# The norm of x in a fused block: its squares behind the casts of V's weights, its additions on Pool

## The chip, the core and the metric

The kernel runs on one core of a Trainium2 chip. The time is the device time of one execution in microseconds. The kernel before took 879.01 us (median of three runs, 878.78 to 880.6). A core has five engines that run side by side, each through its own queue in order: TensorE (matrix products; PE in the profile, with its weight loads as PEld), VectorE (DVE), ScalarE (ACT), GpSimd (Pool, POOL) and SyncE (SP), which here only issues loads. Semaphores make an engine wait for another.

## The reference, cut to what matters

The reference is one layer of a streaming encoder on 512 frames of width 1024, in float32. Two mixers (RWKV-7 and a gated linear recurrence) read one input projection of the normalised x; a cross-attention into a fixed memory of 256 rows and a gated convolutional feed-forward layer follow. What the change touches is at the very front:

```python
def rms_norm(x, g):
    xf = x.astype(jnp.float32)
    y = xf * lax.rsqrt(jnp.mean(xf * xf, axis=-1, keepdims=True) + NORM_EPS)
    return (y * g.astype(jnp.float32)).astype(x.dtype)
...
h = rms_norm(x, norm_mix_g[l])
proj = h @ w_in[l] + b_in[l]
...
kv = m @ w_kv          # m = rms_norm(mem, norm_mem_g[l])
```

The input projection has 38 column blocks of 128 (`w_in`). K and V of the cross-attention depend only on the memory, so the kernel computes them first, while x and its norm are made ready. The low-rank matrices `w_lora_up` and `a_lora_up` are read by the RWKV branch.

## The kernel before, in words

All activations lie transposed: 128 channels on the partitions, frames along the free axis. x is `xraw`, 8 blocks of 128 x 512. Products keep float32 accuracy with three passes of a faster type: every operand is split into a high part (a cast on ScalarE, names ending in `_h` or index 0) and a low part (what the cast left over, a subtraction on VectorE, `_l` or index 1), and `mm3` (L232) multiplies high by high, high by low and low by high into one accumulator.

Weights come in tiles of 128 x 1024 (512 KB). `stream` (L160) issues a load on SyncE's queue, casts the tile on ScalarE (L176) and subtracts on VectorE (L177). There are four buffers for raw tiles and three each for high and low parts, so a load waits for a raw buffer, and everything behind it in SyncE's queue waits too.

The front of the program runs so:

1. The memory `mraw` is loaded, scaled and split into `m2`. K's eight blocks (`k_ps0` to `k_ps7`, 24 products of 256 columns each) are multiplied with eight tiles of `wk`. Two blocks share one accumulator bank, and `k_out` (L415) reads a block from it, scales it by the norm of the memory and hands it to Pool for a store to `dK`. So the last block waits until the block before it has been read.
2. x is loaded in four pieces of two blocks (L428), the pieces standing between weight loads in SyncE's queue. When the norm of the memory is due (after K's block 5), `m_norm` computes it with a refinement step on VectorE (`newton`, L328).
3. The squares of x: ScalarE squares each block (L441, L444), VectorE adds it to `xss` (L445). Two buffers hold squares.
4. V: two halves of 512 columns, each with four tiles of `wv` and 48 products of 512 columns (L465). Between the halves, in program order, stands `x_norm` (L446): `rstd_bc` splits `xss` into two parts (`rx_h`, `rx_l`, by `sum_exact`, L223), sums both over the partitions with a product by ones (`rs_ps`), and ScalarE takes logarithm and exponential to get `rx`, the reciprocal root. Then every block becomes a row of the projection's operand: VectorE multiplies x, its gain and `rx` (L451, `hf32`), ScalarE casts (L452, `h2` high) and VectorE subtracts (L453, `h2` low; `hT` in the profile).
5. The input projection starts with blocks 12 and 13 (L659, L668), whose products run as rows of `h2` come. Between them are the casts and subtractions of two low-rank matrices (L666, L667), which the first low-rank products need much later. A chain of small operations on 128 x 4 tiles (`dp`, L478 to L521) runs on VectorE in the same stretch.

What sets the order: a planner orders each engine's queue before the program runs. It goes through the instructions by program order, with its own idea of how long each takes, and takes what it holds ready. `tc.high_priority()` lets it prefer an instruction, `tc.issue_after(ins)` queues an instruction behind `ins` on the same engine, without a wait for its end, and `tc.keep_in_program_order(ins)` queues it behind everything that was written before it for that engine. The products from input block 4 on follow a list that is written out by hand (`ORDER`); those of K, V and blocks 12 and 13 are the planner's.

Pool's queue holds K's eight stores, one memset (L616), and then the long row of accumulating transfers (`dS`, L551) that add weight quarters for later stages, each of which is let go by a product of the projection.

Of the kernel before, what the change touches and what calls it, by code (L numbers as in the profile page):

```python
# [9 lines left out]
F32 = mybir.dt.float32  # L10
F32R = mybir.dt.float32r
AF = mybir.ActivationFunctionType
ALU = mybir.AluOpType
# [4 lines left out]
P = 128  # L18
T = 512
D = 1024  # L20
KB = D // P
# [58 lines left out]
def hybrid_block_kernel(ctx: ExitStack, tc: tile.TileContext, xT_d, mT_d, pv_d, cst_d, win_d, wk_d, wv_d,  # L80
                        lup_d, gup_d, rga_d, rgx_d, wba_d, wbb_d, wmix_d, wq_d, wo_d, wfi_d, wfo_d, out_d):
    nc = tc.nc
    V, S = nc.vector, nc.scalar
# [65 lines left out]
        return pv[:, o:o + w]  # L149


    wdma, mdma, casts = [], [], []
    OFF = 32

    def weight_tiles(name, g, at):
# [4 lines left out]
    def stream(dram, name, between=None, order=None, at=0):  # L160

        for g in order or range(dram.shape[0]):
            with tc.high_priority():
                raw = wp.tile([P, 1024], F32, tag="wr", name=f"{name}_r{g}", bufs=4)
                n = 512 if len(wdma) < 2 else 1024
                ins = nc.sync.dma_start(raw, dram[g])
                if between is not None:
                    tc.keep_in_program_order(ins)
                    between(0)
                elif len(wdma) == 1:  # L170
                    tc.add_manual_dep(ins.ins, mdma[-1].ins.name, mybir.DependencyInfo(
                        mybir.DependencyClass.NoSync, mybir.DependencyReason.DATA), reason="order of the loads")
                wdma.append(ins)
                hi, lo = weight_tiles(name, g, at)
                for o in range(0, 1024, n):
                    casts.append(S.copy(hi[:, o:o + n], raw[:, o:o + n]))  # L176
                    V.tensor_tensor(lo[:, o:o + n], raw[:, o:o + n], hi[:, o:o + n].bitcast(F32), ALU.subtract)  # L177
                    if between is not None and o == 0:
                        between(1)
                between = None  # L180
            yield hi, lo
# [38 lines left out]
            self.left -= 1  # L220
            return self.hi[:, i * P:(i + 1) * P], self.lo[:, i * P:(i + 1) * P]

    def sum_exact(ps, blocks, src, pool, tag, name):  # L223

        hi = pool.tile(list(src.shape), F32R, tag=tag, name=f"{name}_h", bufs=2)
        lo = pool.tile(list(src.shape), F32R, tag=tag, name=f"{name}_l", bufs=2)
        S.copy(hi, src)
        V.tensor_tensor(lo, src, hi.bitcast(F32), ALU.subtract)
        PE.matmul(ps, blocks, hi, start=True, stop=False)
        PE.matmul(ps, blocks, lo, start=False, stop=True)  # L230

    def mm3(ps, lh, ll, rh, rl, start, stop, **kw):  # L232
        first = PE.matmul(ps, lh, rh, start=start, stop=False, **kw)
        PE.matmul(ps, lh, rl, start=False, stop=False, **kw)
        PE.matmul(ps, ll, rh, start=False, stop=stop, **kw)
        return first
# [99 lines left out]
    def rstd_bc(out, ssq, n, pool=None, scratch=None, load=True, split=None, **kw):  # L336

        ps = rw_ps("rs_ps", pool, **kw)
        if split is None:
            PE.matmul(ps[:, :n], ones, ssq, start=True, stop=True)  # L340
        else:
            sum_exact(ps[:, :n], onesr, ssq, *split)
        rsqrt(out, ps[:, :n], 1.0 / D, eps[:, 0:1], load)
        if scratch is not None:
            newton(out, ps[:, :n], scratch, 1.0 / D, 1e-6)
# [6 lines left out]
    with tc.tile_pool(name="p0", bufs=1, reuse_waits="tile") as p0:  # L352
# [58 lines left out]

        k_ps = []
        last_k = None

        def k_out(m):  # L415
            kt = p0.tile([P, NMEM], F32, tag="kt", name=f"kt{m}", bufs=8)
            ins = V.tensor_tensor(kt, k_ps[m], rm, ALU.mult)
            nc.gpsimd.dma_start(dK[m], kt)
            return ins

        for m in range(KB):
            if m % 2 == 0:
                ps2 = (rw_ps if m == 6 else mm_ps)(f"k_ps{m}")
                k_ps += [ps2[:, :NMEM], ps2[:, NMEM:]]
            (dense_lo_last if m == 1 else dense)(k_ps[m], un, lambda kb: (m2[:, 0, kb, :], m2[:, 1, kb, :]), KB)
            if m >= 4:
                with tc.issue_after(wdma[-1].ins):
                    nc.sync.dma_start(xraw[:, 2 * m - 8:2 * m - 6, :], xT_d[:, 2 * m - 8:2 * m - 6, :])  # L428
            if m == 2:
                m_squares()  # L430
            if m == KNORM:
                m_norm()
                for i in range(m):
                    k_out(i)
            if m >= KNORM:
                last_k = k_out(m)

        xss = p0.tile([P, T], F32, name="xss")
        for k in range(KB):
            if k == 0:  # L440
                S.activation(xss, xraw[:, k, :], AF.Square)  # L441
            else:
                xsq = p0.tile([P, T], F32, tag="xsq", name=f"xsq{k}", bufs=2)
                S.activation(xsq, xraw[:, k, :], AF.Square)  # L444
                V.tensor_tensor(xss, xss, xsq, ALU.add)  # L445
        def x_norm():  # L446
            rx = p0.tile([P, T], F32, name="rx")
            rstd_bc(rx, xss, T, prg, split=(p0, "xsq", "rx"), tag="rg")
            for k in range(KB):
                hf32 = p0.tile([P, T], F32, tag="hf32", name=f"hf32_{k}", bufs=2)  # L450
                V.scalar_tensor_tensor(hf32, xraw[:, k, :], par("nmix", k), rx, ALU.mult, ALU.mult)  # L451
                S.copy(h2[:, 0, k, :], hf32)  # L452
                V.tensor_tensor(h2[:, 1, k, :], hf32, h2[:, 0, k, :].bitcast(F32), ALU.subtract)  # L453

        st = stream(wv_d, "wv", at=OFF)
        for hf in range(2):
            pss = [(mm_ps if hf else rw_ps)(f"v_ps{hf}_{i}") for i in range(2)]
            for k2 in range(4):
                wh, wl = next(st)
                for kk in range(2):  # L460
                    kb = 2 * k2 + kk
                    rh, rl = wh[:, kk * T:(kk + 1) * T], wl[:, kk * T:(kk + 1) * T]
                    for i in range(2):
                        sl = slice(i * P, (i + 1) * P)
                        mm3(pss[i], m2[:, 0, kb, sl], m2[:, 1, kb, sl], rh, rl, kb == 0, kb == KB - 1)  # L465
            if hf == 0:
                x_norm()
            for i in range(2):
                vt = p0.tile([P, T], F32, tag="vt", name=f"vt{hf}_{i}", bufs=2)
                S.activation(vt, pss[i], AF.Copy, scale=rmc[:, i:i + 1])  # L470
                nc.scalar.dma_start(dV[i, :, hf * T:(hf + 1) * T], vt)
# [190 lines left out]
    for i in range(2):  # L662
        hs, oh = half[i], half[1 - i]
        S.copy(pwa[i][hs], twpa[hs])
        V.tensor_tensor(pwa[i][oh], twpa[hs], pwa[i][hs].bitcast(F32), ALU.subtract)
        S.copy(lhi[:, i], lraw[i])  # L666
        V.tensor_tensor(llo[i], lraw[i], lhi[:, i].bitcast(F32), ALU.subtract)  # L667
    evac_shift(inproj(13), 13, sgx)  # L668
    tab(sgx, sgx, AF.Sigmoid)

# [955 lines left out]
```

## Time and profile before

| what | value |
|---|---|
| median of three runs | 879.01 us |
| profiled execution | 879.42 us |
| its span | 877.6 us |
| TensorE busy | 855.6 us (97%) |
| VectorE, ScalarE, Pool busy | 679.5, 514.0, 132.5 us |
| V's first product, first product of the projection | 28.32 us, 55.49 us |

The profile is of one execution. The span runs from the first to the last instruction; the profiled execution's own time is 1.8 us longer. A row of the view in order of time gives start, duration, engine, line, operation, output and inputs, shape and count; in brackets stands how long the engine was idle before it and what ended that. A row of the grouped view gives busy time in all, the mean duration in ns, and idle time ahead of the group. `L95` is the helper through which every product goes, so products are told apart by their tiles. Matrix products overlap, so the distance between starts is their price, not the duration.

### The profile page before, as it was taken

The numbers are of one execution on the slowest core, as the hardware profiler recorded it, in microseconds if no ns is written. First come the engines' busy times: TensorE is split into PE (matmuls) and PEld (weight loads), VectorE is DVE, ScalarE is ACT, GpSimd is POOL, SyncE is SP. The second block draws the span as 40 slices with busy tenths as digits, with TensorE's granted clock in tenths as the row PEclk, the third lists the DMA queues.
The fourth block names the chain that finished last, engine by engine and source line by source line (L and its number), as shares of the span: only waits on it lengthen the run. The fifth ranks groups of instructions, "written<-read, shape, count | busy, mean of one in ns | idle before, by whom it ended". The sixth has DMA issues, their size and how long they took to land.

```text
span 877.6 us, 19313 instructions
## 1 busy us (share of the span) xinstructions
PE 855.6 (97%) x7884; PEld 825.9 (94%) x7884; DVE 679.5 (77%) x1096; ACT 514.0 (59%) x788; POOL 132.5 (15%) x163
## 2 busy tenths in 40 slices
PE   9999989999999999999999999999999999999996
PEld 8889989999997789999999899999999999999996
DVE  6796598877967686685575568799888888999774
ACT  7575676743437687234454356666666566867563
POOL 0102223021101022001122211102111121111100
PEclk9999999999999999999999999999999999999999
DMA  8888799777895479858987858999999999998953
GB/s 284 298 263 220 202 229 232 202 198 242 241 259 138 73 169 265 219 172 223 235 232 168 207 148 201 248 274 276 298 263 293 293 266 305 262 295 212 304 183 96
DMA packets 97576, 201.60 MB, mean 230 GB/s; under 512 B 19600, under 2 KB 30992, under 8 KB 97424
## 3 DMA queue, kind: packets, MB, share of 16 engines
q1 hardware_dynamic: 62240, 118.57, 40.2%
q0 software_dynamic: 25504, 67.38, 37.6%
q10 hardware_dynamic: 9744, 14.42, 4.9%
q8 instruction: 62, 1.02, 0.5%
q14 instruction: 26, 0.21, 0.1%
HBM read 188.54 MB, written 78.12 MB: 304 GB/s over the span
## 4 chain that ended last, share of the span: by engine, by line
PE 74%; DVE 13%; ACT 5%; DMA 4%; issue 3%; DVEq 0%; ACTq 0%; SPq 0%
PE fx_ps L95 14%; PE in_ps L95 13%; PE fyz_ps L95 10%; PE ox_ps L95 7%; PE oyz_ps L95 5%; PE co_ps L95 5%; PE mix_ps L95 4%; PE q_ps L95 4%; PE yb_ps L95 2%; DVE win_l L177 2%; PE v_ps L95 2%; PE o_ps L95 1%; PE k_ps L95 1%; DVE Zt L821 1%; DVE zz L820 1%
## 5 line engine op out<-in xcount | busy, mean ns | idle before, releaser
L95 PE MATMUL in_ps<-hT,win_h 128*128 128x256 f32 x1216 | 214.8, 280 | 2.1 <-DVE pr L655 1.6
L95 PEld LDWEIGHTS in_ps<-hT,win_h 128*128 128x128 f32 x1216 | 185.1, 188 | 6.1 <-DVE pr L655 1.8
L95 PE MATMUL in_ps<-hT,win_l 128*128 128x256 f32 x608 | 170.2, 280 | 1.1 <-DVE win_l L177 1.1
L199 ACT CAST wfi_h<-wfi_r 128x1024 fp32r<-128x1024 f32 x77 | 80.9, 1051 | 69.7 <-PE fyz_ps L95 25.2
L95 PEld LDWEIGHTS in_ps<-hT,win_l 128*128 128x128 f32 x608 | 114.2, 188 | 3.2 <-DVE win_l L177 1.7
L551 POOL DMA_DIRECT2D dS<-in_wfi x66 | 66.8, 1032 | 304.3 <-PE in_ps L95 127.5
L200 DVE TENSOR_TENSOR wfi_l<-wfi_r,wfi_h 128x1024 fp32r<-128x1024 f32 x77 | 94.1, 1222 | 19.8 <-ACT wfi_h L199 19.8
L177 DVE TENSOR_TENSOR win_l<-win_r,win_h 128x1024 fp32r<-128x1024 f32 x38 | 46.3, 1221 | 25.5 <-ACT win_h L176 25.2
L587 POOL DMA_DIRECT2D dOs<-in_wfo x54 | 39.9, 820 | 168.0 <-PE fx_ps L95 45.8
L95 PE MATMUL fx_ps<-hq,wfi_h 128*128 128x256 f32 x352 | 61.2, 276 | 0.0
L95 PE MATMUL fx_ps<-hr,wfi_h 128*128 128x256 f32 x352 | 61.1, 276 | 0.0
L95 PE MATMUL fyz_ps<-hq,wfi_h 128*128 128x256 f32 x352 | 61.1, 276 | 0.0
L95 PE MATMUL ox_ps<-go,wfo_h 128*128 128x256 f32 x352 | 59.9, 276 | 0.0
L176 ACT CAST win_h<-win_r 128x1024 fp32r<-128x1024 f32 x38 | 39.7, 1045 | 34.1 <-PE in_ps L95 31.1
L1436 DVE TENSOR_TENSOR wfo_l<-wfo_r,wfo_h 128x1024 fp32r<-128x1024 f32 (+1 forms) x39 | 47.2, 1213 | 11.6 <-ACT wfo_h L1435 11.6
L1435 ACT CAST wfo_h<-wfo_r 128x1024 fp32r<-128x1024 f32 (+1 forms) x39 | 40.4, 1036 | 25.1 <-DMA wfo_r<-dOs 8.2
L95 PEld LDWEIGHTS fx_ps<-hr,wfi_h 128*128 128x128 f32 x352 | 53.1, 188 | 0.2 <-ACT sn L1371 0.2
L95 PEld LDWEIGHTS fx_ps<-hq,wfi_h 128*128 128x128 f32 x352 | 53.2, 188 | 0.0
L95 PEld LDWEIGHTS fyz_ps<-hq,wfi_h 128*128 128x128 f32 x352 | 53.1, 188 | 0.0
L95 PEld LDWEIGHTS ox_ps<-go,wfo_h 128*128 128x128 f32 x352 | 52.9, 188 | 0.0
L95 PE MATMUL fyz_ps<-hq,wfi_l 128*128 128x256 f32 x176 | 48.7, 277 | 0.6 <-DVE wfi_l L200 0.6
L95 PE MATMUL fx_ps<-hq,wfi_l 128*128 128x256 f32 x176 | 48.6, 276 | 0.0
(392 smaller groups left out, 2337.0 us busy)
## 6 DMA issues: line engine op xcount, KB each, us to landing
dS<-in_wfi POOLq DMA_DIRECT2D x66, 512.0 KB, 8.3
wfi_r<-dS SPq DMA_DIRECT2D x44, 512.0 KB, 7.1
win_r<-in_win SPq DMA_DIRECT2D x38, 512.0 KB, 5.5
wfi_r<-in_wfi SPq DMA_DIRECT2D x33, 512.0 KB, 7.2
dS<-dS POOLq DMA_DIRECT2D x22, 512.0 KB, 5.2
dOs<-in_wfo POOLq DMA_DIRECT2D x12, 512.0 KB, 8.4
wk_r<-in_wk SPq DMA_DIRECT2D x8, 512.0 KB, 5.2
wv_r<-in_wv SPq DMA_DIRECT2D x8, 512.0 KB, 5.2
```

The costliest lines, as they stand in the source:

```text
L95: return self.log(out, nc.tensor.matmul(out, *args, **kw))
L176: casts.append(S.copy(hi[:, o:o + n], raw[:, o:o + n]))
L177: V.tensor_tensor(lo[:, o:o + n], raw[:, o:o + n], hi[:, o:o + n].bitcast(F32), ALU.subtract)
L199: S.copy(hi, raw)
L200: V.tensor_tensor(lo, raw, hi.bitcast(F32), ALU.subtract)
L551: return lambda: nc.gpsimd.dma_start(s(out), src, **kw)
L587: yield lambda k=k, w=w, src=src: nc.gpsimd.dma_start(dO[n, m][:, k * P:(k + w) * P], src, **kw)
L820: V.tensor_tensor(t3, Zt[:, s + 1:, s + 1:], Nm[:, s:s + 1, s + 1:].to_broadcast([P, n, n]), ALU.mult)
L821: V.tensor_reduce(Zt[:, s + 1:, s:s + 1], t3, AX.X, ALU.add)
L1435: S.copy(hi[:, :n], raw[:, :n])
L1436: V.tensor_tensor(lo[:, :n], raw[:, :n], hi[:, :n].bitcast(F32), ALU.subtract)
```

## The change

- `x_squares` takes the place of the loop after K: it is called behind each of the four tiles of V's first half for two blocks of x. Its squares are queued on ScalarE behind that tile's cast, and the seven additions are made by Pool instead of VectorE. Three buffers hold squares.
- The load of V's fifth tile is queued behind x's last piece on SyncE.
- K's eight stores are issued by Pool behind the last of these additions.
- The norm of x runs at high priority, and the first product of its sum is pinned behind V's first half on TensorE.
- The casts and subtractions of the two low-rank matrices are queued behind the last normalised row's cast and subtraction.

```diff
--- before.py
+++ after.py
@@ -149,7 +149,7 @@
         return pv[:, o:o + w]
 
 
-    wdma, mdma, casts = [], [], []
+    wdma, mdma, xdma, casts = [], [], [], []
     OFF = 32
 
     def weight_tiles(name, g, at):
@@ -167,6 +167,9 @@
                 if between is not None:
                     tc.keep_in_program_order(ins)
                     between(0)
+                elif name == "wv" and g == 4:
+                    tc.add_manual_dep(ins.ins, xdma[-1].ins.name, mybir.DependencyInfo(
+                        mybir.DependencyClass.NoSync, mybir.DependencyReason.DATA), reason="order of the loads")
                 elif len(wdma) == 1:
                     tc.add_manual_dep(ins.ins, mdma[-1].ins.name, mybir.DependencyInfo(
                         mybir.DependencyClass.NoSync, mybir.DependencyReason.DATA), reason="order of the loads")
@@ -220,13 +223,13 @@
             self.left -= 1
             return self.hi[:, i * P:(i + 1) * P], self.lo[:, i * P:(i + 1) * P]
 
-    def sum_exact(ps, blocks, src, pool, tag, name):
-
-        hi = pool.tile(list(src.shape), F32R, tag=tag, name=f"{name}_h", bufs=2)
-        lo = pool.tile(list(src.shape), F32R, tag=tag, name=f"{name}_l", bufs=2)
+    def sum_exact(ps, blocks, src, pool, tag, name, bufs=2, pin=lambda ins: ins):
+
+        hi = pool.tile(list(src.shape), F32R, tag=tag, name=f"{name}_h", bufs=bufs)
+        lo = pool.tile(list(src.shape), F32R, tag=tag, name=f"{name}_l", bufs=bufs)
         S.copy(hi, src)
         V.tensor_tensor(lo, src, hi.bitcast(F32), ALU.subtract)
-        PE.matmul(ps, blocks, hi, start=True, stop=False)
+        pin(PE.matmul(ps, blocks, hi, start=True, stop=False))
         PE.matmul(ps, blocks, lo, start=False, stop=True)
 
     def mm3(ps, lh, ll, rh, rl, start, stop, **kw):
@@ -411,11 +414,12 @@
 
         k_ps = []
         last_k = None
+        kts = []
 
         def k_out(m):
             kt = p0.tile([P, NMEM], F32, tag="kt", name=f"kt{m}", bufs=8)
             ins = V.tensor_tensor(kt, k_ps[m], rm, ALU.mult)
-            nc.gpsimd.dma_start(dK[m], kt)
+            kts.append(kt)
             return ins
 
         for m in range(KB):
@@ -425,7 +429,7 @@
             (dense_lo_last if m == 1 else dense)(k_ps[m], un, lambda kb: (m2[:, 0, kb, :], m2[:, 1, kb, :]), KB)
             if m >= 4:
                 with tc.issue_after(wdma[-1].ins):
-                    nc.sync.dma_start(xraw[:, 2 * m - 8:2 * m - 6, :], xT_d[:, 2 * m - 8:2 * m - 6, :])
+                    xdma.append(nc.sync.dma_start(xraw[:, 2 * m - 8:2 * m - 6, :], xT_d[:, 2 * m - 8:2 * m - 6, :]))
             if m == 2:
                 m_squares()
             if m == KNORM:
@@ -436,21 +440,26 @@
                 last_k = k_out(m)
 
         xss = p0.tile([P, T], F32, name="xss")
-        for k in range(KB):
-            if k == 0:
-                S.activation(xss, xraw[:, k, :], AF.Square)
-            else:
-                xsq = p0.tile([P, T], F32, tag="xsq", name=f"xsq{k}", bufs=2)
-                S.activation(xsq, xraw[:, k, :], AF.Square)
-                V.tensor_tensor(xss, xss, xsq, ALU.add)
+
+        def x_squares(ks):
+            for k in ks:
+                xsq = p0.tile([P, T], F32, tag="xsq", name=f"xsq{k}", bufs=3) if k else xss
+                with tc.issue_after(casts[-1].ins):
+                    S.activation(xsq, xraw[:, k, :], AF.Square)
+                if k:
+                    add = nc.gpsimd.tensor_tensor(xss, xss, xsq, ALU.add)
+            return add
+
         def x_norm():
             rx = p0.tile([P, T], F32, name="rx")
-            rstd_bc(rx, xss, T, prg, split=(p0, "xsq", "rx"), tag="rg")
+            with tc.high_priority():
+                rstd_bc(rx, xss, T, prg, split=(p0, "xsq", "rx", 3, tc.keep_in_program_order), tag="rg")
             for k in range(KB):
                 hf32 = p0.tile([P, T], F32, tag="hf32", name=f"hf32_{k}", bufs=2)
                 V.scalar_tensor_tensor(hf32, xraw[:, k, :], par("nmix", k), rx, ALU.mult, ALU.mult)
-                S.copy(h2[:, 0, k, :], hf32)
-                V.tensor_tensor(h2[:, 1, k, :], hf32, h2[:, 0, k, :].bitcast(F32), ALU.subtract)
+                hs = (S.copy(h2[:, 0, k, :], hf32),
+                      V.tensor_tensor(h2[:, 1, k, :], hf32, h2[:, 0, k, :].bitcast(F32), ALU.subtract))
+            return hs
 
         st = stream(wv_d, "wv", at=OFF)
         for hf in range(2):
@@ -463,8 +472,13 @@
                     for i in range(2):
                         sl = slice(i * P, (i + 1) * P)
                         mm3(pss[i], m2[:, 0, kb, sl], m2[:, 1, kb, sl], rh, rl, kb == 0, kb == KB - 1)
+                if hf == 0:
+                    add = x_squares((2 * k2, 2 * k2 + 1))
             if hf == 0:
-                x_norm()
+                for k, kt in enumerate(kts):
+                    with tc.issue_after(add.ins):
+                        nc.gpsimd.dma_start(dK[k], kt)
+                last_h = x_norm()
             for i in range(2):
                 vt = p0.tile([P, T], F32, tag="vt", name=f"vt{hf}_{i}", bufs=2)
                 S.activation(vt, pss[i], AF.Copy, scale=rmc[:, i:i + 1])
@@ -663,8 +677,10 @@
         hs, oh = half[i], half[1 - i]
         S.copy(pwa[i][hs], twpa[hs])
         V.tensor_tensor(pwa[i][oh], twpa[hs], pwa[i][hs].bitcast(F32), ALU.subtract)
-        S.copy(lhi[:, i], lraw[i])
-        V.tensor_tensor(llo[i], lraw[i], lhi[:, i].bitcast(F32), ALU.subtract)
+        with tc.issue_after(last_h[0].ins):
+            S.copy(lhi[:, i], lraw[i])
+        with tc.issue_after(last_h[1].ins):
+            V.tensor_tensor(llo[i], lraw[i], lhi[:, i].bitcast(F32), ALU.subtract)
     evac_shift(inproj(13), 13, sgx)
     tab(sgx, sgx, AF.Sigmoid)
```

## The prediction

> **What bounds the kernel now.** I read the page's head first, then the busy time by stretch around the changed lines, then the instructions in order of time on TensorE, and from each gap there back through VectorE, ScalarE and the load queue.
>
> ```profile
> span 877.6 us, 19313 instructions
> PE 855.6 (97%) x7884; PEld 825.9 (94%) x7884; DVE 679.5 (77%) x1096; ACT 514.0 (59%) x788; POOL 132.5 (15%) x163
> ```
>
> TensorE is the bound: 22 us of the whole span are idle on it. An edit off TensorE can only win idle or stretched time there, so I look for that time in the stretch that the edit touches, V's products and the first input products.
>
> ```profile
> 28.30:40.30 12.00, 10.83 (x47) 8.14 (x46) 11.73 (x26) 8.02 (x14) 3.29 (x6) 1.00 0.83 283
> 40.30:55.50 15.20, 15.20 (x80) 12.90 (x79) 13.29 (x31) 11.89 (x17) 1.22 (x3) 1.00 0.97 342
> 55.50:65.30 9.80, 9.30 (x78) 8.92 (x76) 9.66 (x21) 5.46 (x9) 1.64 (x2) 1.00 0.60 167
> 65.30:75.00 9.70, 9.70 (x85) 9.70 (x86) 9.04 (x27) 6.96 (x9) 1.91 (x2) 1.00 0.85 182
> ```
>
> Columns: stretch, its length, then busy time and instructions of TensorE, weight loads, VectorE, ScalarE and Pool, the granted clock (1.00 throughout), the DMA share and GB/s. VectorE is nearly full from 28.3 to 40.3 (11.73 of 12.00) and from 55.5 to 65.3 (9.66 of 9.80), just where TensorE idles. In the third stretch 78 products took 9.80 us. At the fourth's pace (9.70 / 85 = 0.114 us each) they need 8.90: **0.9 us are lost there**.
>
> ```profile
> 28.32 0.39 PE L95 MATMUL v_ps<-wv_h,m 128*128 128x512 f32 x1
> 29.38 0.50 PE L95 MATMUL v_ps<-wv_l,m 128*128 128x512 f32 x1 [0.66 <-DVE wv_l L177]
> ...
> 31.79 0.63 PE L95 MATMUL v_ps<-wv_h,m 128*128 128x512 f32 x2
> 32.92 0.50 PE L95 MATMUL v_ps<-wv_l,m 128*128 128x512 f32 x1 [0.50 <-DVE wv_l L177]
> ...
> 40.28 0.40 PE L95 MATMUL k_ps<-m,wk_h 128*128 128x256 f32 x2
> ...
> 43.05 0.62 PE L95 MATMUL v_ps<-wv_h,m 128*128 128x512 f32 x2
> ...
> 43.97 0.39 PE L95 MATMUL rs_ps<-rx_h,onesr 128*128 128x512 f32 x1
> ...
> 44.42 0.40 PE L95 MATMUL v_ps<-wv_h,m 128*128 128x512 f32 x1
> ...
> 55.49 0.40 PE L95 MATMUL in_ps<-hT,win_h 128*128 128x256 f32 x2
> ...
> 65.29 0.38 PE L95 MATMUL in_ps<-hT,win_h 128*128 128x256 f32 x1 [0.50 <-DVE hT L453]
> ```
>
> V's second half is 48 products by the code; from 44.42 to 55.49 they take 11.07 us (0.231 each). K's last block took 43.05 - 40.28 = 2.77. V's first half and that block stand between 28.32 and 43.97 = 15.65 us and need 11.07 + 2.77 = 13.84: **1.81 us are lost**. Two gaps make 1.50 of it: 29.38 instead of 28.32 + 0.23 = 28.55 (0.83), and 32.92 instead of 31.79 + 0.46 = 32.25 (0.67). Both wait for the low half of a V tile.
>
> ```profile
> 25.96 0.63 ACT L441 ACTIVATE xss<-xraw 128x512 f32<-128x512 f32 x1 [2.88 <-DMA xraw<-in_xT]
> ...
> 27.02 1.04 ACT L176 CAST wv_h<-wv_r 128x1024 fp32r<-128x1024 f32 x1
> ...
> 29.92 1.03 ACT L176 CAST wv_h<-wv_r 128x1024 fp32r<-128x1024 f32 x1
> ...
> 34.95 0.64 ACT L444 ACTIVATE xsq<-xraw 128x512 f32<-128x512 f32 x1 [1.47 <-DMA xraw<-in_xT]
> ...
> 38.63 1.05 ACT L176 CAST wv_h<-wv_r 128x1024 fp32r<-128x1024 f32 x1 [1.28 <-PE v_ps L95]
> ...
> 42.36 0.62 ACT L227 CAST rx_h<-xss 128x512 fp32r<-128x512 f32 x1 [2.67 <-DVE xss L445]
> ...
> 48.39 0.63 ACT L297 ACTIVATE rx<-rx 128x512 f32<-128x512 f32 x1
> ```
>
> ScalarE stands 2.88 us in front of the first square, because x's first piece is not there; the first V cast is queued behind two squares (25.96 to 27.02, 0.53 each).
>
> ```profile
> 28.09 1.23 DVE L177 TENSOR_TENSOR wv_l<-wv_r,wv_h 128x1024 fp32r<-128x1024 f32 x1 [0.25 <-ACT wv_h L176]
> ...
> 31.64 1.22 DVE L177 TENSOR_TENSOR wv_l<-wv_r,wv_h 128x1024 fp32r<-128x1024 f32 x1
> ...
> 43.01 0.69 DVE L228 TENSOR_TENSOR rx_l<-xss,rx_h 128x512 fp32r<-128x512 f32 x1 [0.74 <-ACT rx_h L227]
> ```
>
> The second V cast ended at 30.95, yet its subtraction began at 31.64: VectorE was busy with other queued work, additions of squares among it.
>
> **The change, part by part.**
>
> *Squares behind the casts.* Each pair now follows a V cast. The first cast starts at 25.96 at the latest (the time at which x's first piece let ScalarE go on), ends at 27.00, its subtraction at 28.3; it is needed at 28.55. So the 0.83 goes. Two squares (1.06) then follow each cast (1.04): 2.10 us on ScalarE per tile, against 12 x 0.231 = 2.77 on TensorE, so the casts keep pace. The second cast, 29.1 at the latest (27.00, two squares, about 1 us of queued norm work), gives a low half at 31.4; it is needed at 28.32 + 2.77 + 0.23 = 31.32. I take the 0.67 as gone too, with up to 0.1 left.
>
> *Additions to Pool.* Off VectorE go seven instructions:
>
> ```profile
> L445 DVE TENSOR_TENSOR xss<-xss,xsq 128x512 f32<-128x512 f32 x7 | 4.8, 687 | 2.8 <-ACT xsq L444 2.8
> ...
> L451 DVE SCALAR_TENSOR_TENSOR hf<-xraw,pv,rx 128x512 f32<-128x512 f32 x8 | 5.7, 746 | 0.0
> L453 DVE TENSOR_TENSOR hT<-hf,hT 128x512 fp32r<-128x512 f32 x8 | 5.3, 682 | 0.0
> ...
> L331 DVE TENSOR_TENSOR rmt<-rmt,rm 128x256 f32<-128x256 f32 x1 | 0.4, 426 | 0.1
> ```
>
> Pool has no addition of this size in the trace; the nearest row, and Pool's DMA issues:
>
> ```profile
> L1506 POOL TENSOR_TENSOR xr<-xr,ro 128x256 f32<-128x256 f32 x2 | 1.4, 720 | 55.0 <-ACT ro L1503 55.0
> ...
> L418 POOL DMA_DIRECT2D dK<-kt x8 | 4.5, 570 | 39.9 <-DVE rmt L331 36.0 <-DVE dp L480 3.4 <-DVE kt L417 0.6
> ```
>
> For twice the columns the price lies between 0.72 (all fixed) and 1.44 (all by size), 5.0 to 10.1 us for seven. I take 1.44: no row separates a fixed part. The pairs of squares end at about 27.1, 30.7, 33.3 and 36.1 (casts at tile ends: 31.1, 33.9; each plus 2.1). Pool then adds 27.2 to 28.6; 30.2 to 33.1; 33.1 to 36.0; 36.0 to 38.9. The high cast (0.62) and its subtraction (0.69) put rx_l at 40.3, where it was 43.70. The sum's two products are pinned behind V's first half, at 28.32 + 13.84 = 42.16 on TensorE if K's block stays inside that half: a margin of 1.9 us, cost 0. At 0.72 the margin is larger; without cover the wait is the price itself, as in the rivals.
>
> *x's last piece sooner; the wait of V's fifth tile behind it.*
>
> ```profile
> 24.75 0.43 SPq L428 DMA_DIRECT2D xraw<-in_xT  x1
> ...
> 29.35 0.33 SPq L166 DMA_DIRECT2D wv_r<-in_wv  x1
> 29.73 0.43 SPq L428 DMA_DIRECT2D xraw<-in_xT  x1
> ...
> DMA to landing us min/median/max: 5.1/6.3/6.6
> ```
>
> The last piece stood behind a V load that waited for a buffer until 29.35. It can go at 25.2 and lands by 31.8 (6.6 at worst) instead of 34.95. Its squares now come behind the fourth cast, at about 35: alone this part wins nothing, and it loses nothing. The V load behind it goes at its old time or earlier; its cast is at 36.6 to 38.6.
>
> *K's stores behind the additions.*
>
> ```profile
> 63.26 0.95 POOL L616 MEMSET rg<- 128x1024 f32 x1 [18.39 <-DVE dp L509]
> ```
>
> Eight issues of 0.57 (4.5 us) now follow Pool's last addition, from 38.9 to about 43.4. Behind them in that queue stands this memset, with 18 us of idle time in front of it: cost 0. Their 1 MB (eight tiles of 128 x 256 floats) moves some 3 us at 342 GB/s; if it fell in front of an input tile it would cost VectorE's split of that tile as much, but the tiles ahead are V's, loaded by then.
>
> *Norm at high priority, low-rank casts last.* rx ended at 49.02, 5 us behind its sum, as casts lay between. Now two activations (0.63 each by that row) and at worst some queued cast follow its sum (42.6): about 44.5. The rows' 16 instructions on VectorE (11.0 us busy) start some 4.5 us earlier, in V's second half, where VectorE has 15.20 - 13.29 = 1.9 us free and two casts less are in ScalarE's way. The two low-rank casts and subtractions only change place: at about 0.53 and 0.69 each they cost 2.4 us if uncovered, but stand behind the last row, where ScalarE is busy for 5.46 of 9.80. The 0.9 us of the input products then shrinks; bounds 0 to 0.9, I take 0.7, since the order of products on TensorE is fixed by a planner whose times differ from these.
>
> *Sum.* 0.83 + 0.67 + 0.2 (of the other 0.31) + 0.7 = 2.4. From the profiled execution's 879.42 this leaves **877.0**. Its own time is 0.4 above the median of 879.01; I keep the 877.0 for the median too, as the forecast lies nearer the upper end of what can be won (1.81 + 0.9 = 2.7, hence 876.7).
>
> **The rivals.**
>
> *Pool and VectorE exclude each other.* Beside the memset above stand these rows:
>
> ```profile
> 64.17 0.73 POOL L551 DMA_DIRECT2D dS<-in_wfi  x1
> ...
> 63.42 0.82 DVE L511 TENSOR_SCALAR dp<-dp 128x4 f32<-128x4 f32 x1
> ...
> 64.55 0.69 DVE L453 TENSOR_TENSOR hT<-hf,hT 128x512 fp32r<-128x512 f32 x1
> ```
>
> A four-column VectorE operation took 0.82 us and ended at 64.24, when Pool's memset ended (64.21); the two-input operation at 64.55 beside Pool's DMA issue took its usual 0.69. No row has a two-input VectorE operation beside a Pool addition, so an exclusion there can neither be read nor denied. If they take turns, VectorE's subtractions (four of 1.22) and four Newton steps (about 0.4 each) push Pool's chain, 10.1 + 6.5 from 27.2, to 43.8; rx_l comes at 45.1 and TensorE stands 2.9 us at 42.16, or less where it already waited for a low half. I take 2.4 in all: 879.42 - 2.4 + 2.4 = 879.4, from 877.8 (an addition of 1.2) up to 880.
> The Trainium skill, "SBUF — State Buffer", section "SBUF: two separate sides", states just this: a shared port pair is held for a whole instruction, by a GpSimd operation or by a VectorE one with two SBUF inputs if the GpSimd one reads SBUF. The memset row agrees with the lock; its clause on two inputs no row here shows. The Trainium skill's "GPSIMD Engine Reference", section "Performance versus the Vector engine", has a two-input addition at 1.96 times VectorE, an estimate of 1.35 us here, and the sum above stands by it.
>
> *The rows gain nothing.* VectorE was busy for 13.29 + 9.66 = 23 of the 25 us from 40.3 to 65.3, so an earlier rx may leave the input products waiting as before: 879.42 - 1.7 = 877.7; with only the first gap won, 878.6.
>
> *Slower: the pinned sum in front of K's last block.* If the planner puts that block behind the sum, TensorE reaches it at 28.32 + 11.07 = 39.4. With turns, rx_l at 45.1 costs 5.7 us there against the 2.7 to be won: 882.4; with additions of 1.2 the chain is 1.7 shorter: 880.7. I take 881.5. It decides once rx_l is later than 39.4 + 2.7 = 42.1. Against it: K's block needs VectorE's early work, which gets emptier, so it should move forward.
>
> **How the numbers follow.** Forecast 0.52 (876.4 to 877.9), taking turns 0.22, rows gain nothing 0.15, slower 0.11. From no change I can tell 0.2%, 1.76 us: below 877.25 is faster, above 880.77 slower. Faster: 0.85 of the forecast (0.44), a fifth of the next two (0.07): 0.51. Slower: 0.8 of the last (0.09), and a tenth of the second (0.02): 0.11. The rest, 0.38, is same. The range goes down to 875.6 (all 2.7 and about 1 us of a changed order in later stages) and up to 879.8, into the second case.
>
> **What would show it.** Right: no gap ahead of V's low-half products, seven Pool additions of about 1.4 us ending near 39, the sum's products without a wait, rx_l near 40 and input products starting near 53.7. Wrong: subtractions or additions stretched where both engines work (turns), a TensorE gap ahead of rs_ps, or a gap at hT as before.

## The result and the profile after

The changed kernel takes **885.12 us** (median; 884.34 to 886.02), the kernel before beside it 879.77 (878.78 to 881.57): ratio 1.0059, 95% interval 1.0046 to 1.0072. It is slower by about 5.3 us, where 877.0 was forecast and the range ended at 879.8. The profiled execution took 884.66 us; here is the head of its page.

```profile
span 882.9 us, 19310 instructions
PE 857.5 (97%) x7884; PEld 827.9 (94%) x7884; DVE 681.0 (77%) x1089; ACT 514.8 (58%) x788; POOL 143.0 (16%) x170
```

The span is 5.3 us longer. TensorE was busy 1.9 us longer with the same 7884 products, and VectorE 1.5 us longer although seven additions (4.8 us) had been taken off it. So instructions were stretched on both. The same stretches as before the change, and two short ones inside them (after the granted clock come the DMA share and GB/s):

```profile
28.30:40.30 12.00, 7.75 (x34) 5.46 (x32) 11.79 (x18) 6.31 (x9) 9.99 (x7) 1.00 0.62 228
40.30:55.50 15.20, 15.08 (x71) 13.12 (x72) 11.95 (x43) 9.11 (x12) 5.79 (x10) 0.89 0.84 278
55.50:65.30 9.80, 9.34 (x57) 8.16 (x55) 9.80 (x14) 6.70 (x10) 0.73 (x1) 1.00 0.72 216
...
40.00:42.00 2.00, 1.58 (x7) 1.58 (x8) 2.00 (x4) 1.25 (x2) 2.00 (x4) 0.59 0.36 141
42.00:44.00 2.00, 2.00 (x12) 2.00 (x11) 0.38 (x1) 0.65 (x1) 2.00 (x4) 0.56 0.88 227
```

The loss lies in the first two stretches. From 28.3 to 40.3 TensorE did 34 products instead of 47, while VectorE was busy for 11.79 us with 18 instructions instead of 26. Then TensorE ran at a granted clock of 0.59 and 0.56 in the two slices from 40 to 44 us. TensorE's instructions in order of time name what it waited for:

```profile
28.66 0.39 PE L95 MATMUL v_ps<-wv_h,m 128*128 128x512 f32 x1
...
32.90 0.49 PE L95 MATMUL v_ps<-wv_l,m 128*128 128x512 f32 x1 [1.08 <-DVE wv_l L180]
...
38.26 0.50 PE L95 MATMUL v_ps<-wv_l,m 128*128 128x512 f32 x1 [2.31 <-DVE wv_l L180]
...
40.42 0.80 PE L95 MATMUL k_ps<-m,wk_h 128*128 128x256 f32 x2 [0.98 <-DVE kt L421]
...
44.85 0.63 PE L95 MATMUL v_ps<-wv_h,m 128*128 128x512 f32 x2
...
49.24 0.39 PE L95 MATMUL rs_ps<-rx_h,onesr 128*128 128x512 f32 x1
...
60.75 0.40 PE L95 MATMUL in_ps<-hT,win_h 128*128 128x256 f32 x2
```

The gap ahead of V's first low-half product is gone, as forecast. Three larger ones stand in its place, 4.37 us by the trace's idle times, each behind VectorE, and K's last block took 44.85 - 40.42 = 4.43 us instead of 2.77. From V's first product to the first input product are 32.09 us instead of 27.17: **4.92 us longer**, which is most of the 5.3 us. The same stretch on VectorE:

```profile
28.33 1.47 DVE L335 TENSOR_TENSOR rmt<-rmt,rm 128x256 f32<-128x256 f32 x1
...
31.11 1.74 DVE L180 TENSOR_TENSOR wv_l<-wv_r,wv_h 128x1024 fp32r<-128x1024 f32 x1
32.77 1.24 DVE L334 TENSOR_TENSOR rmt<-rmt,rmc 128x2 f32<-128x2 f32 x1
33.94 0.41 DVE L421 TENSOR_TENSOR kt<-k_ps,rm 128x256 f32<-128x256 f32 x1
34.27 1.11 DVE L335 TENSOR_TENSOR rmt<-rmt,rmc 128x2 f32<-128x2 f32 x1
...
35.64 1.10 DVE L336 TENSOR_SCALAR rmt<-rmt 128x2 f32<-128x2 f32 x1
...
36.99 1.21 DVE L180 TENSOR_TENSOR wv_l<-wv_r,wv_h 128x1024 fp32r<-128x1024 f32 x1
38.13 1.25 DVE L337 TENSOR_TENSOR rmc<-rmc,rmt 128x2 f32<-128x2 f32 x1
...
41.70 0.68 DVE L231 TENSOR_TENSOR rx_l<-xss,rx_h 128x512 fp32r<-128x512 f32 x1
```

The same kinds of steps in the kernel before:

```profile
36.05 0.15 DVE L331 TENSOR_TENSOR rmt<-rmt,rmc 128x2 f32<-128x2 f32 x1
36.12 0.42 DVE L417 TENSOR_TENSOR kt<-k_ps,rm 128x256 f32<-128x256 f32 x1
...
36.86 0.16 DVE L333 TENSOR_SCALAR rmt<-rmt 128x2 f32<-128x2 f32 x1
```

Four Newton steps on 128 x 2 elements took 1.10 to 1.25 us each, as long as the subtraction of a whole V tile. Three of them have two inputs in SBUF; the fourth (`TENSOR_SCALAR`) has one tensor and constants. `kt<-k_ps,rm`, between them, kept its 0.41: one of its two inputs lies in PSUM (the accumulator banks of TensorE). Pool in the same time:

```profile
28.23 1.29 POOL L450 TENSOR_TENSOR xss<-xss,xsq 128x512 f32<-128x512 f32 x1 [27.77 <-ACT xsq L448]
30.47 6.25 POOL L450 TENSOR_TENSOR xss<-xss,xsq 128x512 f32<-128x512 f32 x4 [0.95 <-ACT xsq L448]
37.46 3.24 POOL L450 TENSOR_TENSOR xss<-xss,xsq 128x512 f32<-128x512 f32 x2 [0.74 <-ACT xsq L448]
40.64 3.96 POOL L480 DMA_DIRECT2D dK<-kt  x7
```

One addition alone took 1.29 us; four in a row took 6.25, two 3.24, so Pool waited as well. This looks like a turn by turn of whole instructions (the halved additions below test it), and VectorE's queue, in order, passes each wait on to what stands behind it.

### The profile page after: what moved, and what is told of

The parts are those of the page before. It is cut to its first block, busy times and chain, and to the rows that moved or that the text cites. A ratio compares the mean times of both kernels' runs of the same rounds, so it can differ in the third digit from the quotient of the medians.

```text
span 882.9 us, 19310 instructions
## 1 busy us (share of the span) xinstructions
PE 857.5 (97%) x7884; PEld 827.9 (94%) x7884; DVE 681.0 (77%) x1089; ACT 514.8 (58%) x788; POOL 143.0 (16%) x170
## 4 chain that ended last, share of the span: by engine, by line
PE 76%; DVE 13%; ACT 5%; DMA 3%; issue 2%; ACTq 0%; DVEq 0%
PE in_ps L95 14%; PE fx_ps L95 14%; PE fyz_ps L95 10%; PE ox_ps L95 7%; PE oyz_ps L95 5%; PE co_ps L95 5%; PE mix_ps L95 4%; PE q_ps L95 4%; PE k_ps L95 2%; PE yb_ps L95 2%; DVE win_l L180 2%; PE o_ps L95 1%; PE sc_ps L95 1%; DMA win_r<-in_win 1%; DVE Zt L837 1%
```

## The experiments

Two theories were put against each other. **T**: a Pool addition and a VectorE instruction with two SBUF inputs exclude each other, and the lost time follows from that. **R**: the new order (squares behind casts, pinned sum, low-rank casts last) is what costs. Every ratio below is against the kernel before, run beside the experiment on the same chip.

### Additions on VectorE, all else as changed

```diff
-                    add = nc.gpsimd.tensor_tensor(xss, xss, xsq, ALU.add)
+                    add = V.tensor_tensor(xss, xss, xsq, ALU.add)
```

> The changed kernel with its seven additions back on VectorE, all else of the change kept (the planner may place the sum's products elsewhere). Theory T (a Pool addition and a VectorE operation with two inputs in SBUF exclude each other, and every such VectorE operation can cost up to a whole Pool addition): no VectorE operation in the stretch takes more than 1.3 us, the small Newton steps take 0.16 again, no TensorE gap over 1 us between 28 and 50, granted clock 1.00 throughout, 877.5 to 880.5 us. Rival R (the loss is from the order: squares behind the casts, the pinned sum, casts of the low-rank matrices last): still 883 to 886 us.

Measured: 878.36 us, ratio 0.9989 (0.9978 to 0.9999). It was run a second time, last of all:

> e1 once more, the changed kernel with its additions on VectorE, beside the three above and for a narrower interval against before. Both theories as measured: 878.4 us, ratio 0.9985 to 0.9995, faster than before and than the changed kernel.

Measured: 878.51 us, ratio 0.9980 (0.9968 to 0.9992). The first two stretches of the first of these runs:

```profile
28.30:40.30 12.00, 12.00 (x67) 10.34 (x66) 11.35 (x25) 7.85 (x11) 4.37 (x8) 1.00 0.94 321
40.30:55.50 15.20, 15.20 (x74) 12.40 (x74) 13.61 (x31) 12.25 (x18) 1.82 (x3) 1.00 0.82 283
```

No idle time on TensorE, 67 products in the first stretch, the clock at 1.00. The change's rules of order are all still there, and the time is 6.5 to 6.6 us below the changed kernel's, each median taken against the kernel before beside it. So the rules alone do not cost, and R falls. Some places moved with the edit: K's last block comes two products later, the sum of squares seven products into V's second half, and K's stores go out from 31.60 on, as their tiles come. The memset experiment below leaves all of these as in the changed kernel. This version is also faster than the kernel before, by 0.1 to 0.2%.

### Additions on Pool, all else as before

```diff
-                V.tensor_tensor(xss, xss, xsq, ALU.add)
+                nc.gpsimd.tensor_tensor(xss, xss, xsq, ALU.add)
```

> The kernel before with only the seven additions moved to Pool, nothing else of the change. T: the same stretched VectorE operations (Newton steps of 1.1 to 1.3 us in place of 0.16), TensorE gaps of 1 to 2.5 us in V's first half, 881 to 885 us. R: 878.5 to 880.5 us, as without the change.

Measured: 886.71 us, ratio 1.0081 (1.0066 to 1.0096). VectorE's instructions there, in order of time:

```profile
30.24 1.21 DVE L331 TENSOR_TENSOR rmt<-rmt,rm 128x256 f32<-128x256 f32 x1
31.48 1.41 DVE L332 TENSOR_TENSOR rmt<-rmt,rm 128x256 f32<-128x256 f32 x1
32.92 1.25 DVE L333 TENSOR_SCALAR rmt<-rmt 128x256 f32<-128x256 f32 x1
...
36.09 0.15 DVE L331 TENSOR_TENSOR rmt<-rmt,rmc 128x2 f32<-128x2 f32 x1
```

And TensorE's:

```profile
29.86 0.50 PE L95 MATMUL v_ps<-wv_l,m 128*128 128x512 f32 x1 [1.02 <-DVE wv_l L177]
35.82 0.50 PE L95 MATMUL v_ps<-wv_l,m 128*128 128x512 f32 x1 [2.91 <-DVE wv_l L177]
```

This one edit alone slows the old kernel by at least as much as the whole change does (0.81% against 0.59%; the intervals overlap). Here the additions met the Newton steps of 256 columns (1.21 to 1.41 us instead of 0.29 to 0.43), and the steps of two columns fell into a pause of Pool's additions and took 0.15. Which of these steps is held depends on whether it runs beside an addition, and not on its size.

### Without the small Newton steps

```diff
-            newton(rmc, psc[:, 0:2], rmt[:, 0:2], 1.0 / D, 1e-6)
```

This kernel leaves out the correction of the two-column reciprocal root that scales V: five VectorE instructions with some 0.8 us of work.

> The changed kernel without the five refinement steps of 128x2 (the memory's norm per row, used to scale V, keeps only the first estimate from logarithm and exponential). They are 0.8 us of work. T: four of them cost 4.7 us on VectorE beside Pool's additions, so the low half of V's third tile and K's last block come 3 to 4 us earlier, the gap of 2.3 us shrinks under 1 us, the clock stays at 1.00, and the time is 880.5 to 882.5 us. R: no more than the 0.8 us, 884 to 885.5 us.

Measured: 881.89 us, ratio 1.0026 (1.0017 to 1.0036): 3.0 us less than the changed kernel, each against the kernel before beside it, from 0.8 us of work. TensorE's waits up to the input products:

```profile
32.64 0.50 PE L95 MATMUL v_ps<-wv_l,m 128*128 128x512 f32 x1 [1.08 <-DVE wv_l L180]
...
45.50 0.50 PE L95 MATMUL v_ps<-wv_l,m 128*128 128x512 f32 x1 [0.76 <-DVE wv_l L180]
```

The gap of 2.31 us is gone and the granted clock is 1.00 throughout. The gap of 1.08 stands behind a subtraction that Pool held (1.89 us). The one of 0.76 has another path: its subtraction took its usual 1.23, but the cast ahead of it came late, because `rx_h`, with a table load of 1.28 us behind it, stood in front of it in ScalarE's queue and had waited 3.62 us for Pool's last addition. So the cost of such a step is the wait, not its work.

### A Pool instruction that reads nothing

```diff
+        acc = p0.tile([P, 1360], F32, name="xss")
+        xss = acc[:, :T]
...
-                    add = nc.gpsimd.tensor_tensor(xss, xss, xsq, ALU.add)
+                    add = nc.gpsimd.memset(acc, 8.0)
+                    tc.add_manual_dep(add.ins, sq.ins.name, mybir.DependencyInfo(
+                        mybir.DependencyClass.Sync, mybir.DependencyReason.DATA), reason="with the square")
```

Each addition becomes a memset of about the same length; the sum of squares is left out.

> The changed kernel with each Pool addition replaced by a Pool memset of 128x1360, which waits for the same square and takes about as long (1.3 us by the 0.95 us of 128x1024); the sum of squares is left out, so the norm of x is that of a constant. TensorE's order up to the projection is the changed kernel's. T, if only a Pool operation that reads SBUF holds a two-input operation: Newton steps with two inputs take 0.16 and 0.42 again, only the tensor-with-constant steps are held for up to a memset, no TensorE gap over 1.2 us, 878 to 881 us. T, if any Pool operation holds VectorE, and R too: 884 to 886 us. The Trainium skill, "SBUF — State Buffer", section "SBUF: two separate sides", states the first of these.

Measured: 878.17 us, ratio 0.9981 (0.9972 to 0.9991). Pool's instructions:

```profile
30.26 2.53 POOL L451 MEMSET xss<- 128x1360 f32 x2 [1.00 <-ACT xsq L449]
```

VectorE's beside them:

```profile
30.37 1.22 DVE L180 TENSOR_TENSOR wv_l<-wv_r,wv_h 128x1024 fp32r<-128x1024 f32 x1
31.51 0.15 DVE L334 TENSOR_TENSOR rmt<-rmt,rmc 128x2 f32<-128x2 f32 x1
...
32.31 0.50 DVE L336 TENSOR_SCALAR rmt<-rmt 128x2 f32<-128x2 f32 x1
```

Beside 2.53 us of memsets a subtraction kept its 1.22 and a Newton product its 0.15; only the instruction of tensor and constants was held (0.50). A Pool busy with memsets is harmless to two-input work; a Pool busy with additions is not. TensorE's products up to the projection stand in the changed kernel's order here, and K's stores go out behind the last memset as there behind the last addition: so the order does not cost, and the additions do. That additions and memsets differ is the clause of the Trainium skill, "SBUF — State Buffer", section "SBUF: two separate sides", which the forecast quoted and had no row for: a two-input VectorE instruction takes the shared ports only against a GpSimd one that reads. The traces now agree on both sides of it: 1.24 us beside an addition, 0.15 beside a memset. That it is the reading which matters, and no other difference between the two, is the skill's statement; the runs compare only these two.

### Additions cut in half

```diff
-                    add = nc.gpsimd.tensor_tensor(xss, xss, xsq, ALU.add)
+                    for h in (slice(0, 256), slice(256, T)):
+                        add = nc.gpsimd.tensor_tensor(xss[:, h], xss[:, h], xsq[:, h], ALU.add)
```

> The changed kernel with each of Pool's seven additions of 128x512 cut into two of 128x256 of some 0.65 to 0.75 us. Theory (VectorE's instruction with two SBUF inputs waits for the end of the Pool instruction that runs): the five small Newton steps take up to 0.7 us each instead of 1.10 to 1.25, the two gaps of TensorE before the last block of K shrink from 3.3 to about 1.5 us, the granted clock stays at 1.00, and the time falls to about 882 us. Rival (the two share the port's rate, so that each slows the other in proportion to what it moves): the small steps, which move next to nothing, take the same 1.1 to 1.25 us or less evenly spread, the Pool work is the same, and the time stays at 885 us or rises.

Measured: 883.49 us, ratio 1.0036 (1.0024 to 1.0048). VectorE's small steps:

```profile
32.04 0.69 DVE L334 TENSOR_TENSOR rmt<-rmt,rmc 128x2 f32<-128x2 f32 x1
...
32.98 0.44 DVE L335 TENSOR_TENSOR rmt<-rmt,rmc 128x2 f32<-128x2 f32 x1
...
35.80 0.69 DVE L337 TENSOR_TENSOR rmc<-rmc,rmt 128x2 f32<-128x2 f32 x1
```

TensorE's longest wait in this stretch:

```profile
35.94 0.50 PE L95 MATMUL v_ps<-wv_l,m 128*128 128x512 f32 x1 [0.72 <-DVE wv_l L180]
```

The held steps shrink with the length of one Pool instruction (0.44 to 0.69 us instead of 1.10 to 1.25), though Pool's total work grew. That fits a lock on whole instructions, and not a rate that is shared. The three gaps fell to 0.53, 0.72 and 0.40 us and the clock stayed at 1.00. The time fell by less than expected (883.49 instead of 882): Pool's chain ended later (41.62 against 40.70), and the waits for rows grew from 0.87 us to 1.57, at 60 to 63 us.

### A forced gap of TensorE, short and long

In the kernel before, the first product of `in_ps9` waits for memsets of Pool (two of 128 x 512, or five), which wait for the last product of `in_ps8`. Nothing else is edited.

```diff
+        if i in (8, 9):
...
+            if i == 9:
+                tc.add_manual_dep(mm[0], held[0].ins.name, sync, reason="hold")
+            else:
...
+                for _ in range(2):
+                    held.insert(0, nc.gpsimd.memset(fill, 0.0))
+                tc.add_manual_dep(held[-1].ins, mm[-1].name, sync, reason="hold")
```

> The kernel before with one forced idle time of TensorE and nothing else: the first product of in_ps9 waits for two memsets of 128x512 by Pool, which wait for the last product of in_ps8; the order of the products, of VectorE, ScalarE and SP is that of before. Estimate of the gap from the 0.95 us of the 128x1024 memset in before: 2 x 0.48 plus signalling, 1.0 to 1.4 us. Theory that a long gap also lowers the granted clock: e3's gap of 1.08 kept 1.00, so no drop here, 879.5 + 1.2 = 880.7 us. Rival, a gap costs only itself: the same 880.7. A gap that costs more than 1.6 us would speak for a drop after short gaps too.

> As the short one with five memsets, a gap of 2.4 to 2.8 us. Theory: the gap is as long as those of the changed kernel (2.31 before the last block of K) and of the kernel before with Pool's additions (2.91), so the granted clock falls to some 0.55 for about 4 us and the kernel loses another 1.6 to 1.9 us: 879.5 + 2.6 + 1.7 = 883.8 us. Rival, a gap costs only itself, and the low clock after those gaps had another cause (the work of the other engines there): 882.1 us and a granted clock of 1.00 behind it.

Measured: short 882.96 us, ratio 1.0032 (1.0018 to 1.0047); long 884.14 us, ratio 1.0044 (1.0028 to 1.0061). The short gap on TensorE:

```profile
96.59 0.50 PE L95 MATMUL in_ps<-hT,win_h 128*128 128x256 f32 x2 [1.22 <-POOL fill L659]
```

The stretch in which it ends:

```profile
96.00:98.00 2.00, 1.41 (x12) 1.41 (x13) 1.63 (x2) 1.02 (x2) 0.90 (x2) 1.00 0.15 61
```

The long gap on TensorE:

```profile
98.45 0.80 PE L95 MATMUL in_ps<-hT,win_h 128*128 128x256 f32 x2 [2.97 <-POOL fill L659]
```

The stretches behind it:

```profile
98.00:100.00 2.00, 1.55 (x7) 1.55 (x8) 0.65 (x2) 1.25 (x2) 0.42 (x2) 0.51 0.63 176
100.00:102.00 2.00, 2.00 (x14) 2.00 (x14) 0.40 (x1) 0.00 (x0) 0.68 (x1) 0.64 0.47 170
102.00:104.00 2.00, 2.00 (x20) 2.00 (x19) 0.00 (x0) 0.00 (x0) 0.00 (x0) 1.00 0.50 182
```

After 1.22 us the clock stays at 1.00; after 2.97 us it is 0.51 and 0.64 in the next two slices, about 3 us of slow products. The first product of the low-rank block (`psw`), 5 to 7 us later, starts 1.8 us later than in the kernel before with the short gap and 5.1 us later with the long one: 1.75 us more of gap cost 3.3. So the low clock follows from the gap alone and costs about 1.5 us. End to end the two versions lie only 1.2 us apart and their intervals overlap, so this price rests on the traces. The Trainium skill, "TensorE: Matmul & The Clock Gate", section "What's actually happening", has half clock after an idle window of about 3.4 us that runs freely, and its section "Why this matters for your kernels" advises against idle times of more than about 3 us. Here 2.97 was enough, and in the changed kernel 2.31 with 0.98 shortly behind it; a single gap of 2.10 us, in the run with the low-rank casts early (below), left the clock at 1.00.

The end-to-end time of the short gap was a miss: 880.7 was expected. Its runs scatter from 880.5 to 885.5, and the profiled one lost some 2 us more between 187 and 282 us, far from the edit. Why is open.

### The sum not pinned

```diff
-                rstd_bc(rx, xss, T, prg, split=(p0, "xsq", "rx", 3, tc.keep_in_program_order), tag="rg")
+                rstd_bc(rx, xss, T, prg, split=(p0, "xsq", "rx", 3), tag="rg")
```

> The changed kernel without the instruction that keeps the sum of x's squares in program order on TensorE (the high priority stays). The planner then puts that sum inside the last block of K, so the rows are written earlier. Theory (Pool's additions hold VectorE, and TensorE's gaps follow from that): gaps and low clock stay; only the two waits for rows of 0.46 and 0.41 us at 64 and 66 us go, and the sum may cost the K block a gap of its own: 883.5 us, rows' first product some 6 us earlier. Rival (the place of the sum is what costs): 877 to 879.5 us.

Measured: 883.78 us, ratio 1.0045 (1.0028 to 1.0061). The sum's products start at 44.0 instead of 49.2, the waits for rows are gone, and the gaps of 1.07, 2.32 and 0.97 us and the low clock (0.50 and 0.68) stay; `psw` starts at 104.6 instead of 106.2. The pin costs 1.2 to 1.6 us here (by the ratios and by `psw`; the intervals of the ratios overlap); Pool's additions cost the rest.

### The other parts one by one

Squares behind the casts alone, on the kernel before, with the additions on VectorE:

```diff
+                with tc.issue_after(casts[-1].ins):
+                    S.activation(xsq, xraw[:, k, :], AF.Square)
+                if k:
+                    V.tensor_tensor(xss, xss, xsq, ALU.add)
...
+                if hf == 0:
+                    x_squares((2 * k2, 2 * k2 + 1))
```

> The kernel before with one part of the change: x's squares queued behind the casts of V's tiles, pair by pair; the additions stay with VectorE, and the early piece of x, the pinned sum, the low-rank casts and the K stores stay as before. Forecast's step, the two gaps of TensorE of 0.83 and 0.67 us before V's later tiles come from the squares: both gone, 879.7 - 1.5 = 878.2 us, first product of the low-rank block some 1.5 us earlier than in before (98.8 against 100.3). Rival, the gaps come from VectorE's load or from the transfers: gaps stay, 879.7 us.

Measured: 880.72 us, ratio 1.0005 (0.9992 to 1.0018): no gain, where 878.2 was the forecast's step; the reason is read below. Without the early piece of x, on the version with VectorE's additions:

```diff
-                elif name == "wv" and g == 4:
-                    tc.add_manual_dep(ins.ins, xdma[-1].ins.name, mybir.DependencyInfo(
-                        mybir.DependencyClass.NoSync, mybir.DependencyReason.DATA), reason="order of the loads")
```

> The changed kernel with its additions on VectorE (as in e1) and without the earlier reading of x's last piece. Forecast's step, that piece wins nothing: the same as e1 within 0.3 us, 878.4 us, and the first products of the rows at 53.8 us as in e1. Rival, the early piece is what lets the squares follow the casts: the sum's products come 1 to 2 us later, and the time rises to 879.5 us.

Measured: 878.71 us, ratio 0.9988 (0.9977 to 0.9999). On the same version, low-rank casts without their place behind the rows:

```diff
-        with tc.issue_after(last_h[0].ins):
-            S.copy(lhi[:, i], lraw[i])
-        with tc.issue_after(last_h[1].ins):
-            V.tensor_tensor(llo[i], lraw[i], lhi[:, i].bitcast(F32), ALU.subtract)
+        S.copy(lhi[:, i], lraw[i])
+        V.tensor_tensor(llo[i], lraw[i], lhi[:, i].bitcast(F32), ALU.subtract)
```

> The changed kernel with its additions on VectorE (as in e1) and without the rule that queues the low-rank casts behind the normalised rows. Forecast's step, those casts ahead of the rows cost up to 0.7 us in the first input products: 878.4 + 0.7 = 879.1 us, with waits for rows or weights at 55 to 66 us that e1 has not. Rival, the order of the low-rank casts is worth nothing: 878.4 us.

Measured: 881.16 us, ratio 1.0021 (1.0005 to 1.0036), 2.65 us above the version with that rule beside it. ScalarE's instructions there:

```profile
44.65 0.62 ACT L680 CAST lhi<-lraw 128x512 fp32r<-128x512 f32 x1 [2.23 <-DMA lraw<-in_lup]
45.17 1.04 ACT L179 CAST wv_h<-wv_r 128x1024 fp32r<-128x1024 f32 x1
46.12 0.61 ACT L230 CAST rx_h<-xss 128x512 fp32r<-128x512 f32 x1
```

TensorE's wait:

```profile
46.78 0.49 PE L95 MATMUL rs_ps<-rx_h,onesr 128*128 128x512 f32 x1 [2.10 <-ACT rx_h L230]
```

The low-rank cast waits for a transfer, and the sum's high half stands behind it. The wait is not at 55 to 66 us, where it was expected, but ahead of the sum. TensorE with the squares alone:

```profile
46.52 0.50 PE L95 MATMUL rs_ps<-rx_h,onesr 128*128 128x512 f32 x1 [1.74 <-ACT rx_h L227]
```

It is the same wait (the cast stood 1.87 us): the two gaps between V's products are gone, and the sum's wait has taken their place. The early piece of x is worth nothing that can be measured.

## Why the prediction was wrong

The first products of three stages, from the traces (us), show where each version stood:

| kernel | V | first input product | `psw` | span |
|---|---|---|---|---|
| before | 28.3 | 55.5 | 100.3 | 877.6 |
| changed | 28.7 | 60.8 | 106.2 | 882.9 |
| additions on VectorE | 28.4 | 53.8 | 98.0 | 874.7 |
| the same, second run | 28.8 | 54.2 | 98.4 | 877.4 |
| Pool writes only | 28.5 | 54.1 | 99.1 | 876.7 |
| squares alone | 28.5 | 55.9 | 100.3 | 877.7 |

**The step that failed** is "Additions to Pool". It took Pool's time for its only price, with "a margin of 1.9 us, cost 0", as if the additions ran beside VectorE. Pool's addition itself was sized well (1.29 us alone; 1.44 was taken), and the sum's low half, ready at 42.38 instead of 40.3, was 2.1 us late without anyone waiting for it. What was missed is the other side of the lock: VectorE's waits, and behind them 4.37 us of TensorE's gaps and 1.66 us of low clock.

**The rival that took turns was the right mechanism with a wrong price.** Its range ended at 880, 5 us short. It charged 2.4 us, all through Pool's chain and the wait of the sum's products. That wait did not occur at all: the products ran at 49.24, where rx_l had been there since 42.38. The price came by a path that the forecast did not follow: a step of 128 x 2 elements costs up to a whole addition; VectorE's queue hands that on to the low halves and to `kt`; TensorE stands 4.37 us; and the gap brings the low clock. Added up, gaps 4.37 and K's block 4.43 - 2.77 = 1.66 make 6.0; less the 1.16 (0.66 and 0.50) idle in the trace of before, 4.9, which is the 4.92 that was measured. The chance given to it, 0.22, rested on "No row has a two-input VectorE operation beside a Pool addition". That was true, and the memset row beside it, where the held step has one tensor and constants, was no evidence on this case: with memsets in the additions' place such steps are held and the two-input ones are not.

**The slower rival** named the pinned sum in front of K's last block. The order was the other one, the block ahead of the sum, so its mechanism did not occur. The pin did cost something, 1.2 to 1.6 us, by holding the sum behind V's late products.

**The steps on the V gaps held.** With the additions on VectorE, from V's first product to the first input product are 25.4 us, 1.7 less than before; 1.7 was forecast. From there to `psw` are 44.2, 0.65 less; 0.7 was forecast. `psw` starts 2.3 us earlier (1.9 in the second run): up to there the 2.4 of the sum came out, in a kernel whose additions stay on VectorE. But the medians of that version are only 1.2 and 1.3 us better: between `psw` and the first product of `vr` (at 274.3 us before) single executions differ by 2 us and more (172.4 and 174.8 us in its two traces, 174.0 before). How much of a gain outlives that stretch is not settled.

**The parts are not separable**, as the sum took them to be. Squares behind the casts alone win nothing, since the low-rank cast then stands in front of the sum and waits for its transfer. The rule that puts it last, costed inside the 0.7 as a change of place, is worth 2.65 us by the medians once the squares have moved. The forecast counted those casts by their work, 0.53 each, and not by the arrival of their input (a wait of 2.23 us).

**x's last piece** wins nothing, as forecast. **K's stores** were issued from 40.64 on with no one waiting behind them, as forecast.

## What to carry to other kernels

Before moving work to Pool, list what VectorE does in the same microseconds: each of its instructions with two SBUF inputs, however small, can cost a whole Pool addition, and whatever stands behind it in VectorE's queue is late by as much. Beside Pool's memsets, which read nothing, the two-input steps kept their time, and beside its additions the step with an operand in PSUM did. A step of one tensor with constants was held by both (0.50 us beside a memset instead of 0.16). When parts of an edit are costed one by one, ask of each instruction that moves when its input arrives, since a queue in order makes everything behind it wait for that too.

## What the runs showed of the hardware that was not expected

That a step's price depends on its neighbour and hardly on its size: the same 128 x 2 product took 0.15 us beside a memset and 1.24 beside an addition of 1.29, more than eight times as much. And that a single wait of some 3 us on TensorE is paid for one and a half times, the second part as about half a clock for some 3 us of products behind it.
